# Three paddings in SBUF: where a kernel's streamed weight blocks and one operand buffer start

## Chip, cores and metric

The kernel runs on one NeuronCore of a Trainium2 chip. The metric is the device time of one execution in microseconds (us); a change is judged by runs of the kernels before and after on the same chip.

## The reference, cut to what matters

A batch of one sequence of 256 tokens, 2048 wide, passes through two blocks in float32:

```
x = first_block(x):    proj = rmsnorm(x) @ w_in                 # 2048 x 9264
                       pooled branch, sparse attention, gated merge, @ w_out
x = second_block(x):   z = rmsnorm(x) @ w_in_2                  # 2048 x 6160
                       forgetting attention + mLSTM, @ w_out_2
                       x = x + peer_ffn(rmsnorm(x))
peer_ffn:              scores = x @ w_q ...; the 16 best of 128*128 experts, 8 heads
                       act = gelu(u[idx] . x) * gate ; y = sum(act * v[idx])
```

Nearly all of the work is products of the 256 tokens with weight matrices that are read once from HBM. The expert tables `peer_u` and `peer_v` (16384 x 2048 each) are read in full: the kernel computes `gelu(x @ u.T)` for every expert, multiplies by a gate table that is zero for experts that were not chosen, and multiplies by `v`.

## The kernel before

**Arithmetic.** A float32 operand is split into a high part (an fp32r copy, made on ScalarE, line 159) and a low part (the difference, made on VectorE, line 160), and a product is three matmuls: high x high, high x low, low x high.

**Streamed blocks.** Every weight matrix comes in blocks of 128 partitions x 1024 float32 (4096 bytes in each partition, 512 KB in all). `stream()` loads one into a `wr` tile, splits it into `wh` and `wl`, and hands these to TensorE. The tiles lie in the pool "stream" (4 `wr`, 3 `wh`, 3 `wl`), and from the expert part on (line 1104, from about 1370 us) also in a second pool, "stream2": of each five blocks two then go to stream2. The pools are plain stacks in a partition, so the size of what is allocated ahead of a tile decides the address at which it starts.

**Consumers.** There are three loops over streamed blocks:

- `dense_half` (line 210; the outputs are named `mm` and `qp`): the 128x128 weights are the stationary operand, the tokens' operand (256 columns, in the big tiles `S0` to `S5`, named `S` in the profile, or in `ypp` for the pooled branch) is the moving one. A block gives 24 matmuls: 16 with `wh`, 8 with `wl`. There are 15,360 of them.
- `dense_N` (lines 193 to 195, outputs `mmn`): the tokens are stationary, the weights move, 512 columns. There are 768.
- `v_mm` (lines 1327 and 1331, outputs `y`): the gated activations `ah`, `al` are stationary, the `peer_v` block moves, 512 columns. A block gives 12 matmuls: 8 with `wh`, 4 with `wl`. There are 3072, of which 3024 have a streamed block and 48 a copy in an `S` tile.

Each matmul loads its own stationary operand; the load of the next one runs beside the matmul at hand. Between blocks of `dense_half`, other matmuls are put in: `sc` (routing scores), `rT`, and in the second half of the expert part the `G` pairs (line 1258) that build the gate table.

**Order.** The framework's scheduler orders the instructions. TensorE gets them in one queue, and the streamed blocks are loaded by one DMA queue of SyncE.

**Addresses.** Three tiles exist only to move others, or have columns that are never read: `pad` at the head of pool "stream", `pad2` at the head of the next pool ("sy", which holds `S0`, `S2`, `S3`; everything allocated later lies above it), and the first 16 columns of `ypp`. In the built program the start addresses have these remainders modulo 256 bytes:

| tile | first address before | remainder before |
|---|---|---|
| `wr`, `wh`, `wl` in stream | 21952, 38336, 50624 | 192 |
| `wr`, `wh`, `wl` in stream2 | 127808, 144192, 152384 | 64 |
| `S0` to `S5` (tokens' operands) | 62976 and up | 0 |
| `ah`, `al` (gated activations) | 189248, 199488 | 64 |
| `ypp` (its used part) | 199296 | 128 |

All steps inside these tiles from one matmul to the next are multiples of 512 bytes, so an operand keeps its remainder through a block.

Of the kernel before, what the change touches and what calls it, by code (L numbers as in the profile page):

```python
# [7 lines left out]
F32 = mybir.dt.float32  # L8
F32R = mybir.dt.float32r
# [6 lines left out]
P = 128  # L16
T = 256
# [113 lines left out]
def emit(tc, I, out):  # L131
# [5 lines left out]
    def pool(stack, name, bufs=1, psum=False, **kw):  # L137
        if psum:
            kw["space"] = bass.MemoryType.PSUM
        return stack.enter_context(tc.tile_pool(name=name, bufs=bufs, **kw))  # L140

    cp = pool(es, "const")
    ws = pool(es, "stream")

    pad = ws.tile([P, 16], F32, name="pad")
    nc.gpsimd.memset(pad, 0.0)

    def const(key, pl=None):
# [97 lines left out]
        return r[:, None, :].to_broadcast([r.shape[0], 2, T])  # L246

    sy = pool(es, "sy")
    pad2 = sy.tile([P, 16], F32, name="pad2")
    nc.gpsimd.memset(pad2, 0.0)  # L250
    es_x = ExitStack()
    sx = pool(es_x, "sx")
# [396 lines left out]

    es_m = ExitStack()  # L650
    pm = pool(es_m, "pm")
    ypp = Parts(pm.tile([P, 16 * T + 16], F32R, name="ypp")[:, 16:])
    e8 = slice(0, 8)
    split(yp, ypp.hi(e8), ypp.lo(e8))
    on = parts(2, 4)
# [30 lines left out]
    pm = pool(es_m, "pm2")  # L686
# [727 lines left out]
```

## Time and profile before

| | |
|---|---|
| time, median of 3 runs | 2917.97 us (2916.59 to 2923.99) |
| profiled execution | 2919.02 us, span 2917.2 us |
| TensorE busy | 2879.9 us, 99% of the span, 20,690 matmuls |
| VectorE, ScalarE busy | 1896.0 us (65%), 1563.2 us (54%) |
| granted TensorE clock | 0.997 of full (2.4 GHz), full in nearly every slice |
| DMA | 596 MB, mean 204 GB/s |

The matmuls are pipelined: a matmul's recorded duration (276 to 281 ns with 256 columns) is longer than the distance from its start to the next one's. In what follows, **pace** means that distance: the time between two starts in the timeline, divided by the matmuls between them.

### The profile page before, as it was taken

Reading aid. Unit: us, or ns where it says so; the run is one execution under the profiler, and the core shown is the slowest. Engines: PE = TensorE matmul, PEld = TensorE weight load, DVE = VectorE, ACT = ScalarE, POOL = GpSimd, SP = SyncE. Lnnn points to the kernel's source line nnn. Section 1 sums busy time; section 2 is a strip of 40 time slices with the busy share of each in tenths; the row PEclk is TensorE's granted clock in tenths of the full one; section 3 lists DMA queues with packets and bytes.
Section 4 is the critical chain, followed back from the end, with each engine's and each line's share of the span. In section 5 each row is a group of like instructions: output and inputs, shape, how many; then the busy total and the mean of one; then the engine's idle time right before and its main releaser. Section 6 shows DMA issues by size and latency. Waiting matters only on the chain.

```text
span 2917.2 us, 51579 instructions
## 1 busy us (share of the span) xinstructions
PE 2879.9 (99%) x20690; PEld 2690.4 (92%) x20690; DVE 1896.0 (65%) x2994; ACT 1563.2 (54%) x2463; POOL 80.7 (3%) x92
## 2 busy tenths in 40 slices
PE   8999999999999999998999999999999999999998
PEld 8998999999999899898999999999998888888887
DVE  7665666655557776566887878888645555555554
ACT  5544555544445455555444479999644444444443
POOL 0000223100000000000000000000000000000000
PEclk9999999999999999999999999999999999999999
DMA  6755444455654544444655567676866676776653
GB/s 229 239 197 187 158 151 137 165 187 184 217 186 165 181 161 163 161 160 164 229 199 210 196 238 247 237 253 239 301 226 232 242 248 221 245 247 222 245 189 114
DMA packets 197201, 596.12 MB, mean 204 GB/s; under 512 B 20832, under 2 KB 55008, under 8 KB 192736
## 3 DMA queue, kind: packets, MB, share of 16 engines
q1 hardware_dynamic: 196960, 592.82, 58.4%
q8 instruction: 162, 2.65, 0.4%
q14 instruction: 79, 0.65, 0.1%
HBM read 553.92 MB, written 35.65 MB: 202 GB/s over the span
## 4 chain that ended last, share of the span: by engine, by line
PE 97%; DVE 1%; DMA 1%; ACT 1%; issue 0%; SPq 0%; DVEq 0%; ACTq 0%
PE mm L210 58%; PE y L1327 16%; PE y L1331 8%; PE qp L210 2%; PE mmn L194 2%; PE mmn L195 2%; PE mmn L193 2%; PE G L1258 1%; PE pT L609 1%; DMA wr<-in_w_kcr 0%; PE po L193 0%; PE po L194 0%; DVE kb L405 0%; PE po L195 0%; ACT wh L159 0%
## 5 line engine op out<-in xcount | busy, mean ns | idle before, releaser
L160 DVE TENSOR_TENSOR wl<-wr,wh 128x1024 fp32r<-128x1024 f32 x976 | 1191.6, 1223 | 777.0 <-ACT wh L159 719.2
L159 ACT ACTIVATE wh<-wr 128x1024 fp32r<-128x1024 f32 x976 | 1033.0, 1061 | 1160.8 <-PE mm L210 522.6
L210 PE MATMUL mm<-S,wh 128*128 128x256 f32 x9600 | 1243.3, 280 | 11.2 <-ACT wh L159 9.3
L210 PEld LDWEIGHTS mm<-S,wh 128*128 128x128 f32 x9600 | 1173.6, 188 | 16.7 <-ACT wh L159 10.6
L210 PE MATMUL mm<-S,wl 128*128 128x256 f32 x4800 | 664.4, 279 | 0.0
L210 PEld LDWEIGHTS mm<-S,wl 128*128 128x128 f32 x4800 | 604.4, 188 | 1.8 <-issue 1.0
L1327 PE MATMUL y<-wh,al 128*128 128x512 f32 x1008 | 315.1, 393 | 0.0
L1327 PE MATMUL y<-wh,ah 128*128 128x512 f32 x1008 | 314.8, 393 | 0.0
L1331 PE MATMUL y<-wl,ah 128*128 128x512 f32 x1008 | 274.3, 393 | 0.0
L1327 PEld LDWEIGHTS y<-wh,ah 128*128 128x128 f32 x1008 | 189.1, 188 | 43.7
L1327 PEld LDWEIGHTS y<-wh,al 128*128 128x128 f32 x1008 | 189.2, 188 | 43.6
L1331 PEld LDWEIGHTS y<-wl,ah 128*128 128x128 f32 x1008 | 189.2, 188 | 43.3
L194 PE MATMUL mmn<-wl,S 128*128 128x512 f32 x256 | 102.3, 400 | 1.0 <-DVE wl L160 1.0
L195 PE MATMUL mmn<-wh,S 128*128 128x512 f32 x256 | 101.7, 397 | 0.0
L193 PE MATMUL mmn<-wh,S 128*128 128x512 f32 x256 | 97.2, 399 | 0.0
L1256 ACT ACTIVATE om<-gm,gTl 128x128 fp32r<-128x128 f32 x256 | 94.1, 398 | 0.0
L1256 ACT ACTIVATE om<-gm,gTh 128x128 fp32r<-128x128 f32 x256 | 87.6, 398 | 0.2 <-DVE gm L1248 0.2
L599 POOL TENSOR_SCALAR sm<-sm,ls 128x128 f32<-128x128 f32 (+1 forms) x64 | 77.4, 1225 | 272.5 <-DVE sc L595 143.6
L1262 ACT ACTIVATE gst<-G 128x256 f32<-128x256 f32 x128 | 81.1, 637 | 1.3
L1263 DVE TENSOR_TENSOR gst<-gst,G 128x256 f32<-128x256 f32 x128 | 76.7, 634 | 2.7 <-ACT gst L1262 2.5
L194 PEld LDWEIGHTS mmn<-wl,S 128*128 128x128 f32 x256 | 48.2, 188 | 11.7 <-DVE wl L160 1.4
L195 PEld LDWEIGHTS mmn<-wh,S 128*128 128x128 f32 x256 | 48.2, 188 | 10.6
(463 smaller groups left out, 2042.0 us busy)
## 6 DMA issues: line engine op xcount, KB each, us to landing
wr<-in_peer_u SPq DMA_DIRECT2D x256, 512.0 KB, 3.7
wr<-in_peer_v SPq DMA_DIRECT2D x256, 512.0 KB, 3.9
wr<-in_w_mg SPq DMA_DIRECT2D x64, 512.0 KB, 3.2
wr<-in_w_o SPq DMA_DIRECT2D x64, 512.0 KB, 3.2
wr<-in_w_q SPq DMA_DIRECT2D x32, 512.0 KB, 3.2
wr<-in_w_gn SPq DMA_DIRECT2D x32, 512.0 KB, 3.4
wr<-in_w_no SPq DMA_DIRECT2D x32, 512.0 KB, 3.3
wr<-in_w_pq SPq DMA_DIRECT2D x32, 512.0 KB, 3.2
```

Source lines behind the costliest of these rows:

```text
L159: se.activation(hi, src, AF.Copy)
L160: (eng or ve).tensor_tensor(lo, src, hi.bitcast(F32), op=sub)
L193: te.matmul(out_, ah, bh, start=start, stop=False, skip_group_check=True)
L194: te.matmul(out_, ah, bl, start=False, stop=False, skip_group_check=True)
L195: te.matmul(out_, al, bh, start=False, stop=stop, skip_group_check=True)
L210: te.matmul(pt, (l if i == 2 else h)[:, s], x.lo(kk) if i == 1 else x.hi(kk), start=start and i == 0 and k == 0, stop=stop and i == 2 and ...
L599: nc.gpsimd.tensor_scalar(v, v, ls[:, c:c + 1], None, op0=mult)
L1256: se.activation(om[:, t, P * i:P * i + P], o2[:, t], AF.Copy, scale=gt.bitcast(F32)[:, tk + t:tk + t + 1])
L1262: se.activation(g2, pt[:, :, 0], AF.Copy)
L1263: ve.tensor_tensor(g2, g2, pt[:, :, 1], op=add)
L1327: te.matmul(yb[tt, c + d], a[p][:, ts], w[0][d], start=i == 0 and p == 0, stop=False, **f)
L1331: te.matmul(yb[tt, c + d], a[0][:, ts], w[1][d], start=False, stop=i == P - 1, **f)
```

## The change

It gives the two pad tiles 48 instead of 16 columns, and the unused head of `ypp` 48 instead of 16. Nothing else differs. The built programs have the same instructions in the same order on TensorE, VectorE, ScalarE and SyncE; on GpSimd two memsets of the pads grow from 128x16 to 128x48.

```
-    pad = ws.tile([P, 16], F32, name="pad")
+    pad = ws.tile([P, 48], F32, name="pad")
     nc.gpsimd.memset(pad, 0.0)
...
-    pad2 = sy.tile([P, 16], F32, name="pad2")
+    pad2 = sy.tile([P, 48], F32, name="pad2")
     nc.gpsimd.memset(pad2, 0.0)
...
-    ypp = Parts(pm.tile([P, 16 * T + 16], F32R, name="ypp")[:, 16:])
+    ypp = Parts(pm.tile([P, 16 * T + 48], F32R, name="ypp")[:, 48:])
```

In the built program the tiles of pool "stream" move up by 128 bytes, and everything above by 256 bytes:

| tile | remainder before | remainder after |
|---|---|---|
| `wr`, `wh`, `wl` in stream | 192 | 64 |
| `wr`, `wh`, `wl` in stream2 | 64 | 64 |
| `S0` to `S5` | 0 | 0 |
| `ah`, `al` | 64 | 64 |
| `ypp` | 128 | 0 |

## Rows read from the trace of the kernel before

**Rows 1.** The page's first part: busy time, share of span, instructions.

```profile
PE 2879.9 (99%) x20690; PEld 2690.4 (92%) x20690; DVE 1896.0 (65%) x2994; ACT 1563.2 (54%) x2463; POOL 80.7 (3%) x92
```

**Rows 2.** Longest pieces of the chain: start us, us, what, matmuls.

```profile
183.85 20.74 PE mm L210 x183
...
556.32 283.15 PE mm L210 x2404
840.33 90.69 PE mm L210 x768
989.62 43.24 PE mm L210 x381
...
1387.34 31.14 PE mm L210 x272
...
2070.27 128.16 PE mm L210 x1128
```

**Rows 3.** Timeline of TensorE, two blocks of y: start us, us, line, operation, count.

```profile
2217.66 0.62 PE L1327 MATMUL y<-wh,ah 128*128 128x512 f32 x2
...
2220.45 0.63 PE L1327 MATMUL y<-wh,ah 128*128 128x512 f32 x2
...
2221.37 0.62 PE L1327 MATMUL y<-wh,ah 128*128 128x512 f32 x2
...
2223.18 0.62 PE L1327 MATMUL y<-wh,ah 128*128 128x512 f32 x2
```

**Rows 4.** Windows with TensorE alone: window, length, busy, matmuls, clock, DMA share.

```profile
1400.00:1710.00 310.00, 310.00 (x2711) 1.00 0.59 205
1730.00:2060.00 330.00, 330.00 (x2841) 1.00 0.70 243
2080.00:2190.00 110.00, 110.00 (x973) 1.00 0.77 268
2200.00:2880.00 680.00, 680.00 (x2947) 1.00 0.66 229
```

**Rows 5.** Windows, the matmuls of line 210 alone, in two interrupted stages.

```profile
250.00:550.00 300.00, 229.26 (x1782) 1.00 0.46 154
920.00:1360.00 440.00, 260.57 (x2117) 1.00 0.47 165
```

**Rows 6.** Timeline of TensorE, dense_N with the tokens stationary.

```profile
228.35 0.40 PE L193 MATMUL mmn<-wh,S 128*128 128x512 f32 x1
...
231.62 0.40 PE L195 MATMUL mmn<-wh,S 128*128 128x512 f32 x1
```

**Rows 7.** Timeline of TensorE where G pairs stand between blocks of dense_half.

```profile
2008.72 0.63 PE L1258 MATMUL G<-om,ah 128*128 128x256 f32 x4
2009.19 2.05 PE L210 MATMUL mm<-S,wh 128*128 128x256 f32 x16
2011.08 1.10 PE L210 MATMUL mm<-S,wl 128*128 128x256 f32 x8
2012.02 2.05 PE L210 MATMUL mm<-S,wh 128*128 128x256 f32 x16
...
2018.13 0.64 PE L1258 MATMUL G<-om,ah 128*128 128x256 f32 x4
2018.60 2.00 PE L210 MATMUL mm<-S,wh 128*128 128x256 f32 x16
2020.44 1.07 PE L210 MATMUL mm<-S,wl 128*128 128x256 f32 x8
2021.34 1.98 PE L210 MATMUL mm<-S,wh 128*128 128x256 f32 x16
```

**Rows 8.** Groups by line in 700 to 720 us: count, busy us, mean ns.

```profile
L210 PE MATMUL mm<-S,wh 128*128 128x256 f32 x81 | 10.5, 279 | 0.0
...
L210 PE MATMUL mm<-ypp,wh 128*128 128x256 f32 x32 | 4.1, 281 | 0.0
```

**Rows 9.** The pads on GpSimd: duration ns, first and last start us.

```profile
L146 POOL MEMSET pad<- x1: 111/111/111, 0.7 to 0.7; 128x16 f32 x1
```

## The prediction

> **What bounds the kernel now.** I read the page's first part, then the chain, then the timeline of TensorE. The page shows an engine that is never without work: 2879.9 us busy out of 2917.2, while VectorE stands at 65% and ScalarE at 54% [rows 1]. So no wait can be removed; only the pace of the matmuls can change. The chain shows that this pace is not one number. The same matmul, same shape, same clock, stands there in long unbroken pieces: 20.74 us for 183, which is 113.3 ns each; 283.15 us for 2404, which is 117.8; 90.69 us for 768, which is 118.1; 128.16 us for 1128, which is 113.6 [rows 2]. There are two paces, about 113.3 and 117.8 ns, and a piece keeps its own for hundreds of microseconds. The reader is to see that neither the clock (1.00 in every window [rows 4]) nor waiting makes the difference.
>
> The timeline of the last stage shows two paces side by side. A block of y that lies in pool "stream" starts at 2217.66, the next one, in stream2, at 2220.45, and the one after that, in "stream" again, at 2223.18: 2.79 us against 2.73 us for the same 12 matmuls [rows 3]. In the stream2 block the first four are still slow; the last eight take 1.81 us, 226.3 ns each, against 232.5 ns over the "stream" block. This repeats with the rotation of five blocks all through the stage: 680 us for 2947 matmuls is 230.7 ns, between the two [rows 4]. What tells the two kinds of block apart is the start address: remainder 192 in "stream", 64 in stream2, and the stationary `ah` and `al` at 64.
>
> **The change part by part.** It takes out no instruction and adds none. Two memsets grow threefold; one takes 111 ns at 0.7 us [rows 9], long before the first matmul, and I cost them at nothing; if they did delay something, twice 0.2 us. What moves is the remainder of three quarters of the streamed blocks, from 192 to 64, and of `ypp`, from 128 to 0. The offset of stationary to moving operand then is, in every loop, that of the stream2 blocks today, except in dense_N, where no streamed block has it yet. I go loop by loop; the sum is of (pace today minus fast pace) times matmuls.
>
> *The y stage.* Today 230.7, fast 226.3, over 3024 matmuls: 13.3 us. In all 98 unbroken stream2 blocks of the timeline the pace is down after four matmuls, and in all 148 unbroken "stream" blocks it is up. I take all of it. Bounds: 0 and 13.3.
>
> *dense_half, uninterrupted (556 to 931 us).* 2404 times (117.8 - 113.3) is 10.8 us, 768 times (118.1 - 113.3) is 3.7: ceiling 14.5 us [rows 2].
>
> *dense_half in the expert part.* From 1400 to 1710 us, 310 us for 2711 matmuls is 114.35 ns, 1.05 over the fast pace: 2.8 us. From 1730 to 2060, 330 us for 2841 is 116.2, 2.9 over: 8.2 us [rows 4].
>
> *dense_half between attention parts.* 1782 matmuls from 250 to 550 us and 2117 from 920 to 1360 [rows 5], of which 381 already run at 113.5 [rows 2]; most of the others run at the slow pace in the timeline. At 4.5 ns: 8.0 and 7.8 us at most.
>
> *dense_N.* From 228.35 to 231.62 us there are 14 matmuls: 233.6 ns [rows 6], 7.3 over the 226.3 of the fast y. Over 768: 5.6 us at most. No trace row shows this pairing (tokens at 0 stationary, weights at 64 moving); nearest are the y blocks, one offset fast and one slow, so I take half, 2.8.
>
> The ceilings add up to 60 us. How much of dense_half is got depends on what a remainder of 64 does there, and that is not as plain as in y. The pace is kept: both kinds of block go on at the one they are entered with if it is the fast one, and other matmuls put in between reset it. The rows show three things. After a G pair a stream2 block can stay slow to its end (2009.19: 16 in 1.89 us, 118 ns, then 8 in 0.94), and the next, in "stream", stays slow too; another stream2 block (2018.60) is at 113 by its second half (8 in 0.90), and the next one in "stream" keeps that [rows 7]. Counted over the timeline from 1400 to 2070 us, blocks entered right after `sc`, `rT` or `G` come out fast in 20 of 32 cases in stream2 and in none of 46 in "stream". And `ypp` today, with weights at 192 against 128, has the offset 64 already, and is slow throughout: its blocks (281 ns recorded, beside 279 for those of the same slow piece [rows 8]) lie inside the piece at 556 us [rows 2]. Handed over slow, it stays slow. So 64 gives a way out that 192 does not, but no certain one. I take half where the row nearest is the G pair: 7.2 of 14.5, 4.0 of 8.0, 3.9 of 7.8. After `sc` all 5 of 5 recovered: 2.5 of 2.8. With G pairs at almost every block the pace is drawn anew each time, and the stream2 blocks that today rescue a slow neighbour no longer do so: 2.0 of 8.2. Against this stands the stretch from 2070 us, fast today (1128 matmuls [rows 2]); entered slow and not interrupted, it would cost 1128 x 4.5 = 5.1 us; I charge 0.45 of that, 2.3.
>
> Sum: 13.3 + 7.2 + 2.5 + 2.0 + 4.0 + 3.9 + 2.8 - 2.3 = 33.4 us. The profiled execution took 2919.0 us (span 2917.2 and 1.8 around it), 1 us over the median of the runs; 2918.0 - 33.4 is 2884.6, and I say 2885 us. What must keep up is cover: at the fast pace a block of 512 KB is wanted every 2.72 us, and from 2080 to 2190 us the DMA engines supply just that at 0.77 busy, TensorE without a gap [rows 4].
>
> A rule of the Trainium skill speaks against all this. "SBUF — State Buffer", section "Who interferes with whom", gives TensorE two independent read ports, one for the moving operand and one for the weight load, and says that "PE and ACT never wait on anyone"; by that, addresses that are legal cannot matter, and the sum is 0. The two blocks of rows 3 do not agree with it.
>
> **The rivals.**
>
> *Nothing happens (2909 to 2927 us).* The pace might go with the pool itself (its region of SBUF, or the place of a block in the rotation) and only by chance with the remainder. For: in this trace the remainder and the pool cannot be told apart for y. Against: `ypp` and the 4-block copies in `S` tiles at remainder 0 are slow in yet other regions. A second form is that the gain is eaten by waits; against it stands the window from 2080 us. It gives 2918.
>
> *y alone (2900 to 2909 us).* dense_half falls to the slow pace once, in the long uninterrupted piece as now, and 64 holds it there, as `ypp` shows. Then 13.3 us less something for dense_N: 2918 - 13.3 = 2904.7.
>
> *Everything fast (2858 to 2864 us).* All ceilings: 2918 - 60 = 2858.
>
> *Slower (2927 to 2940 us).* The slow pace sticks at 64 better than at 192. Then what is fast today turns slow: 381 + 1128 matmuls of the chain and some 555 before 210 us, of which 183 are shown, at 4.5 ns: 9.3 us; and 1400 to 1710 us from 114.35 to 117.8, 2711 x 3.45 = 9.4. Together 18.7 us, 2936.7 if y gains nothing. It decides only if y gains less than 10 of its 13.3. For it speaks the block at 2009.19; against, that no stream2 block entered fast ever became slow unless something was put in.
>
> **How the numbers follow.** Within 0.3% (8.8 us) this measurement can hardly tell a change from none. Partial take-up (2864 to 2900, centre 2885): 0.62. Everything: 0.08. y alone: 0.14. Nothing: 0.10. Slower: 0.06. So faster 0.84, same 0.10, slower 0.06. The range 2862 to 2907 leaves out part of "everything", a little of "y alone", and the last two, about 0.2; within the likeliest case alone it would be 2866 to 2899.
>
> **What would show it.** In the profile after, every y block should take 2.72 us, without the alternation of rows 3; that is the firm step. The pieces of the chain at 556 and 840 us should show 113 to 114 ns for a matmul; if they still show 117.8, the piece was entered slow and 64 held it there. The piece after the last G pair (128.16 us for 1128) should not be longer. dense_N at 226 or 233 decides the half I guessed. The prediction is wrong if y blocks stay at 2.79, or if the pace is right and the span does not follow because TensorE starts to wait for blocks.

## The result and the profile after

The changed kernel took 2883.75 us, the median of 4 runs (2882.7 to 2885.67), against 2917.28 us (4 runs, 2915.65 to 2923.99) for the kernel before on the same chip. The ratio is 0.9882, with a 95% interval of 0.9864 to 0.9899. The profiled execution took 2884.6 us, of which 2882.7 are the span.

The page's first part, of the changed kernel:

```profile
PE 2847.4 (99%) x20690; PEld 2673.1 (93%) x20690; DVE 1896.4 (66%) x2994; ACT 1559.9 (54%) x2463; POOL 80.1 (3%) x92
```

The same 20690 matmuls keep TensorE busy for 32.5 us less than in [rows 1], and VectorE's work is unchanged. Outside its busy time TensorE has 35.3 us of the span (2882.7 - 2847.4), against 37.3 before: it does not wait less, it goes faster. The chain of the changed kernel, its longest pieces that answer to [rows 2]:

```profile
181.76 20.76 PE mm L210 x183
...
549.75 272.49 PE mm L210 x2404
823.10 90.69 PE mm L210 x768
971.83 43.25 PE mm L210 x381
...
2043.84 132.85 PE mm L210 x1128
```

Each duration divided by its count is the pace. The piece of 2404 went from 117.8 to 113.3 ns, the piece of 768 stayed at 118.1, and the piece of 1128, fast before at 113.6, is now slow at 117.8. So with one and the same offset, 64, in all of them, dense_half still has its two paces.

Windows of the changed kernel, TensorE alone (length, busy, matmuls, clock, DMA share, GB/s), which answer to [rows 4]:

```profile
1400.00:1710.00 310.00, 310.00 (x2728) 1.00 0.63 209
1730.00:2060.00 330.00, 330.00 (x2849) 1.00 0.73 246
2080.00:2190.00 110.00, 110.00 (x882) 1.00 0.67 228
2200.00:2840.00 640.00, 640.00 (x2826) 1.00 0.70 235
```

y goes at 640 / 2826 = 226.5 ns. The kernel before has 2774 matmuls in the same window, 230.7 ns. The window of 2080 us, still without a gap, now holds the slow piece and the beginning of y. In the stretch with the G products almost nothing was won: 115.8 ns for a matmul against 116.2. The next rows are the matmuls of line 210 alone, in the two stages of [rows 5]:

```profile
250.00:550.00 300.00, 231.07 (x1824) 1.00 0.49 155
920.00:1360.00 440.00, 257.38 (x2117) 0.99 0.50 165
```

The timeline of y, of the changed kernel (start us, us, line, operation, count), no longer alternates as in [rows 3]. Block follows block at 2.72 us, whichever pool the block lies in:

```profile
2214.61 0.62 PE L1327 MATMUL y<-wh,ah 128*128 128x512 f32 x2
...
2217.33 0.62 PE L1327 MATMUL y<-wh,ah 128*128 128x512 f32 x2
...
2220.05 0.62 PE L1327 MATMUL y<-wh,ah 128*128 128x512 f32 x2
```

dense_N, in the timeline, starts its 14 matmuls within 3.20 us, 228.6 ns each against 233.6 in [rows 6]:

```profile
224.87 0.39 PE L193 MATMUL mmn<-wh,S 128*128 128x512 f32 x1
...
228.07 0.39 PE L195 MATMUL mmn<-wh,S 128*128 128x512 f32 x1
```

The timeline around the G products, in the place of [rows 7], shows what has become of dense_half there:

```profile
1997.83 0.63 PE L1258 MATMUL G<-om,ah 128*128 128x256 f32 x4
1998.29 2.05 PE L210 MATMUL mm<-S,wh 128*128 128x256 f32 x16
2000.18 1.10 PE L210 MATMUL mm<-S,wl 128*128 128x256 f32 x8
...
2003.95 0.64 PE L1258 MATMUL G<-om,ah 128*128 128x256 f32 x4
2004.42 2.00 PE L210 MATMUL mm<-S,wh 128*128 128x256 f32 x16
2006.25 1.07 PE L210 MATMUL mm<-S,wl 128*128 128x256 f32 x8
2007.16 1.98 PE L210 MATMUL mm<-S,wh 128*128 128x256 f32 x16
2008.97 1.07 PE L210 MATMUL mm<-S,wl 128*128 128x256 f32 x8
2009.88 0.63 PE L1258 MATMUL G<-om,ah 128*128 128x256 f32 x4
2010.35 2.05 PE L210 MATMUL mm<-S,wh 128*128 128x256 f32 x16
```

From start to start (the recorded ends overlap), the first block behind the first G group takes 1.89 us for 16 matmuls, 118 ns: slow. Behind the second group the 8 of `wl` are down to 0.91 us, and the next block takes 1.81 for 16: fast. The third group is followed by a slow one again (2.05 us in the record, like the first). Counted over the timeline, the 63 pieces of dense_half behind G groups that are long enough to tell go fast, slow, fast, slow, in strict turn (between the first two fast ones stand 7 matmuls alone, at 117.6 ns); the last piece, of 1128, comes as a slow one.

### The profile page after: what moved, and what is told of

Its sections match the earlier page's. It is cut to its first block, busy times and chain, and to the rows that moved or that the text cites. A ratio compares the mean times of both kernels' runs of the same rounds, so it can differ in the third digit from the quotient of the medians.

```text
span 2882.7 us, 51579 instructions
## 1 busy us (share of the span) xinstructions
PE 2847.4 (99%) x20690; PEld 2673.1 (93%) x20690; DVE 1896.4 (66%) x2994; ACT 1559.9 (54%) x2463; POOL 80.1 (3%) x92
## 4 chain that ended last, share of the span: by engine, by line
PE 96%; DVE 2%; DMA 1%; ACT 1%; issue 0%; SPq 0%; DVEq 0%; ACTq 0%
PE mm L210 57%; PE y L1327 16%; PE y L1331 8%; PE qp L210 2%; PE mmn L194 2%; PE mmn L195 2%; PE mmn L193 2%; PE G L1258 1%; PE pT L609 1%; DMA wr<-in_w_kcr 0%; DVE wl L160 0%; PE po L194 0%; PE po L193 0%; DMA rsw<-rraw 0%; ACT wh L159 0%
## 5 line engine op out<-in xcount | busy, mean ns | idle before, releaser
L210 PE MATMUL mm<-S,wh 128*128 128x256 f32 x9600 | 1233.2, 279 | 10.1 <-ACT wh L159 8.1
```

Of the source, the lines that this page charges most:

```text
L210: te.matmul(pt, (l if i == 2 else h)[:, s], x.lo(kk) if i == 1 else x.hi(kk), start=start and i == 0 and k == 0, stop=stop and i == 2 and ...
```

## The experiments

**Offset or address.** The theory: the pace goes with the distance, modulo 256 bytes, between the start of the stationary and of the moving operand ("offset" in all that follows; dense_half has the weights stationary). The rival: it goes with the remainder of the streamed block itself, which the change sets to 64. Three kernels tell them apart, each the kernel before with these paddings:

```
                       pad  pad2  ypp
before                  16    16   16
changed kernel          48    48   48
e1_pad2_ypp             16    48   48
e2_pad_only             48    16   16
e3_no_ypp               48    48   16
```

The first has the changed kernel's offsets, with every remainder 128 bytes away from the changed kernel's:

```
-    pad2 = sy.tile([P, 16], F32, name="pad2")
+    pad2 = sy.tile([P, 48], F32, name="pad2")
-    ypp = Parts(pm.tile([P, 16 * T + 16], F32R, name="ypp")[:, 16:])
+    ypp = Parts(pm.tile([P, 16 * T + 48], F32R, name="ypp")[:, 48:])
```

> pad stays at 16 columns; pad2 and ypp get 48. Streamed blocks of pool stream start at 192 as before, those of stream2 now at 192, S at 128, ah and al at 192, ypp at 128: every absolute remainder differs from the change's, every offset of stationary to moving operand is the change's (64 in dense_half, 0 in y). Theory 1 (the offset sets the pace): 2884 us within 4, all y blocks 2.72 us. Theory 2 (a streamed block must itself lie at 64): no block does, so y runs at 232.5 to 233 ns throughout, 2917 to 2925 us.

It took 2887.46 us (4 runs, 2882.98 to 2890.47); ratio 0.9886, interval 0.987 to 0.9903, the changed kernel's within the measurement. Its chain:

```profile
557.58 272.49 PE mm L210 x2404
830.92 87.29 PE mm L210 x768
...
2049.76 132.85 PE mm L210 x1128
```

and its window of y:

```profile
2200.00:2840.00 640.00, 640.00 (x2825) 1.00 0.71 237
```

The piece of 2404 and the slow last piece are those of the changed kernel to 0.01 us, from other addresses, and y has 2825 matmuls in the window where the changed kernel has 2826 and the kernel before 2774. The piece of 768 is fast here (113.7 ns).

The second moves the streamed blocks to remainder 64 without a change of the offsets that dense_half and y have in the kernel before, since everything behind pool "stream" moves with them:

```
-    pad = ws.tile([P, 16], F32, name="pad")
+    pad = ws.tile([P, 48], F32, name="pad")
```

> Only pad gets 48 columns. Streamed blocks of pool stream start at 64 as in the change, but everything above moves by the same 128 bytes, so every offset is that of before. Theory 1 (the offset sets the pace): 2917 us within 4, y blocks alternate 2.79 and 2.73 us. Theory 2 (a streamed block must itself lie at 64): the blocks in stream are fast, those in stream2 (now at 192) slow; three of five blocks instead of two are fast, 2895 to 2912 us.

It took 2919.16 us (10 runs, 2916.41 to 2924.17); ratio 1.0004, interval 0.9994 to 1.0014. Its windows have 2773 matmuls of y in 640 us (2774 before), and its chain has the piece of 2404 slow and the last one fast, as in [rows 2]:

```profile
555.59 281.50 PE mm L210 x2404
837.95 90.69 PE mm L210 x768
...
2067.63 128.16 PE mm L210 x1128
```

So the rival falls: without a change of offset, moving the blocks to remainder 64 wins nothing in y or in the time. One part does not follow from the offset. The 1.65 us that its first piece is shorter than before are the 384 matmuls on `ypp`, at 113.5 ns here and 117.7 ns in the kernel before (counted over the timeline), with the same offset, 64, in both kernels: at 64 either pace can come. There is one profile of each, so it stays open whether the addresses, which are 128 bytes apart, or the execution decided here.

The third leaves only `ypp` out of the change, so that its matmuls lie at offset 192 amid others at 64:

```
-    ypp = Parts(pm.tile([P, 16 * T + 48], F32R, name="ypp")[:, 48:])
+    ypp = Parts(pm.tile([P, 16 * T + 16], F32R, name="ypp")[:, 16:])
```

> The change without its third line: ypp stays at 128 with the weights at 64, offset 192 for 384 of the 2404 matmuls of the long piece. Theory 1: offset 192 keeps a fast pace that it is entered with, so 2884 us within 3 and the piece at 113.4 ns for a matmul. Rival: the switch of offset inside the piece resets the pace, and the piece after the first ypp block runs at 117.8: up to 10 us slower, 2894 us.

It took 2886.05 us (2884.32 to 2887.44); ratio 0.9885, interval 0.9868 to 0.9901. The piece of 2404 in its chain is 1.76 us longer than the changed kernel's:

```profile
552.80 274.25 PE mm L210 x2404
827.91 87.30 PE mm L210 x768
```

and its timeline shows where:

```profile
700.66 2.05 PE L210 MATMUL mm<-ypp,wh 128*128 128x256 f32 x16
...
703.48 2.04 PE L210 MATMUL mm<-ypp,wh 128*128 128x256 f32 x16
...
706.31 1.98 PE L210 MATMUL mm<-S,wh 128*128 128x256 f32 x16
708.13 1.07 PE L210 MATMUL mm<-S,wl 128*128 128x256 f32 x8
```

The two blocks on `ypp` take 5.65 us for 48 matmuls, 117.7 ns; the block on `S` behind them is fast at once (16 in 1.82 us). All 384 matmuls at 192 are slow in this kernel, and the ones at 64 around them fast. That an offset handed over at the fast pace keeps it, as the prediction had it, is wrong: a change of offset can end the fast pace, and another one brings it back.

**Other offsets.** Is 64 a good offset, or is it only better than 192? Four kernels (s0_offset0, s128, s96, s32) scan it. `pad2` moves the tokens and everything behind them, and a pad at the head of stream2 keeps that pool at the same offset as "stream"; y then has its operands at offset 0, as in the changed kernel. The sizes are 64 and 48 columns for offset 0, 32 and 16 for 128, 40 and 8 for 96, 56 and 56 for 32. For offset 0, against the kernel before:

```
-    pad2 = sy.tile([P, 16], F32, name="pad2")
+    pad2 = sy.tile([P, 64], F32, name="pad2")
     more[:] = [pool(es_e, "stream2", **bt), 4, 2]
+    pad3 = more[0].tile([P, 48], F32, name="pad3")
+    nc.gpsimd.memset(pad3, 0.0)
```

> Weights against tokens' operands at offset 0 in dense_half (pad2 of 64 columns), y blocks against ah and al at 0 (a pad of 48 columns at the head of stream2). Theory 1: y gains its full 13 us as in the change; dense_half at offset 0 has no row so far. If offset 0 is as good in dense_half as it is in y (leaves the slow pace within four matmuls), nearly all of dense_half is fast: 2865 us. If it holds the slow pace: 2900 us or more.

> Offset 128 in every dense_half block that was at 192 before, y and dense_N at offset 0. With offset 0 the 256-column matmuls went at about 120 ns throughout and the kernel took 2957.75 us. Theory A (only the distance from offset 0 counts, 128 is the farthest): dense_half at 113.3 ns nearly everywhere, so the 24 us that the changed kernel still has above that pace are gone: about 2860 us, the chain's 2404-matmul piece 272 us and its 1128-matmul piece 128 us. Theory B (the offset counts modulo 128): about 120 ns throughout again, 288 us and 135 us for the two pieces, about 2956 us. Theory C (64 and 192 are alike and 128 is like them, two paces drawn anew after interruptions): 2880 to 2900 us.

> Offset 96 in dense_half, y and dense_N at 0. If the pace changes gradually with the offset away from 0 and 128, 96 is as good as or better than 64: about 2860 to 2884 us, 2404-matmul piece at most 272.5 us. If a multiple of 64 is what the fast pace needs, 96 goes at 118 to 120 ns throughout: 284 to 288 us for that piece, about 2935 to 2956 us.

> Offset 32 in dense_half, y and dense_N at 0. If the pace changes gradually with the distance from 0: between the 120 ns of offset 0 and the mixture of offset 64, about 2900 to 2950 us. If a multiple of 64 is what counts: like 96, 2935 us or more. If any offset other than 0 does: about 2884 us.

(dense_N, with the tokens stationary, is at the reverse of dense_half's offset: at 0 in the first of the four only, at 128, 160 and 224 in the others, not at 0 as three of these expectations say. The 384 matmuls on `ypp` stand 128 away from the others' offset.)

They took 2957.75, 2949.91, 2941.22 and 2943.36 us, one run each. The piece of 2404 matmuls in their chains, in this order, and of the first also the last piece:

```profile
564.37 287.95 PE mm L210 x2404
...
2114.82 135.36 PE mm L210 x1128
```

```profile
567.04 286.12 PE mm L210 x2404
```

```profile
561.38 285.30 PE mm L210 x2404
```

```profile
564.88 285.06 PE mm L210 x2404
```

That is 119.8, 119.0, 118.7 and 118.6 ns for offsets 0, 128, 96 and 32 in the first piece, and the last piece is slow in all four (135.36, 133.86, 133.86 and 133.48 us). As means of a piece, all are above even the slow pace of 64 and 192, 117.8 ns (single stretches go below it: the `ypp` blocks of s96, at offset 224, take 116.7 ns by the timeline). Of those tried, 113.3 ns is reached for long only at 64 and 192. The theory that only the distance from 0 counts falls (128 would be best), and so does a gradual change from 0 to 64.

The first of them also shows that what is worst for 256 columns is best for 512. In a window of y its matmuls take 226.5 ns, at the very offset at which dense_half takes 119.8:

```profile
2300.00:2840.00 540.00, 540.00 (x2384) 1.00 0.72 240
```

**What turns the pace over.** The changed kernel's last piece is slow at an offset that can be fast. My first thought was the prediction's: an interruption draws the pace anew. Six added matmuls of 128 columns, ahead of that piece and behind the last G group, should draw again (kernel f6_flip, and f6_timed, which is the same once more):

```
         jobs.append((2.6, lambda t4=t4: g_quad(t4)))
+
+    def six():
+        pt = side_bank("six")
+        for a in range(2):
+            mm3(pt[:, P * a:P * a + P], kyh[:, a], kyl[:, a], kyh[:, 1 - a], kyl[:, 1 - a], True, True)
+
+    jobs.append((0.7, six))
```

> The changed kernel's paddings, and six added 128-column matmuls right behind the last pair of G products, ahead of the 1128 matmuls of the last uninterrupted dense_half piece, whose pace is slow in the changed kernel (117.8 ns, 132.85 us). Theory: an interruption draws the pace of what follows anew, and 128-column matmuls were followed by the fast pace in 14 of 15 cases: the piece takes 128.2 us at 113.3 ns, about 4.7 us less, and the kernel about 2880 us (the six matmuls cost under 1 us). Rival: the offset and the blocks of this stage fix the pace, whatever came before: 132.85 us again, and 2884 us.

> The kernel with the six added matmuls once more, timed in rounds: its one look gave 2877.38 us and a 1128-matmul piece of 127.90 us. If that is the piece's gain and no accident, 2876 to 2881 us; if the 768-matmul piece (87.30 us there, 90.69 us in the changed kernel) varies from run to run, up to 3.4 us more in some.

One run gave 2877.38 us; the 4 later ones gave 2882.34 (2880.42 to 2884.04), ratio 0.9871, interval 0.9856 to 0.9886. The two pieces in the chain of the second:

```profile
828.41 90.69 PE mm L210 x768
...
2048.28 127.90 PE mm L210 x1128
```

The last piece is fast both times, 4.95 us shorter than in the changed kernel; so its pace hangs on what stands ahead of it. Whether such matmuls draw, turn over or set the pace, this does not tell. The timelines of the eight profiles with the changed kernel's streamed offset tell it for like matmuls, those of `sc` between 1400 and 1660 us: behind groups of six the pace is fast 96 times of 96, four times from slow, and behind the two groups of five it is turned over each time, from fast to slow 8 times and from slow to fast 8 times. That is no drawing, and six do not turn the pace over there; but the added six have other operands. By the time the gain of the last piece cannot be told from the changed kernel (intervals overlap), because other pieces vary between executions by some microseconds: the piece of 768 is 87.30 us in the first run's profile and 90.69 here. It starts behind a wait of 0.87 us for VectorE's `g`, in all kernels alike, and among the profiles with the changed kernel's offset in it it is slow in two (this one and the changed kernel's own) and fast in all others.

The strict turn behind the G groups speaks against drawing. G's own operands lie at offset 0 in both kernels, amid dense_half at 64. So I moved only them: the tile of `om` is made 64 columns longer and `om` begins at its column 48, while y's `al`, which uses the same buffers, begins at 0. No instruction is added, removed or moved on TensorE. Against the changed kernel (kernel g64):

```
-            om = pv[0].tile([P, 2, T], F32R, tag="al", bufs=GRP // 2 + 1, name="om")
+            om = pv[0].tile([P, 2 * T + 64], F32R, tag="al", bufs=GRP // 2 + 1, name="om")[:, 48:48 + 2 * T].rearrange("p (t c) -> p t c", t=2)
...
-            al = pv.tile([P, 2, T], F32R, tag="al", bufs=GRP // 2 + 1, name="al")
+            al = pv.tile([P, 2 * T + 64], F32R, tag="al", bufs=GRP // 2 + 1, name="al")[:, :2 * T].rearrange("p (t c) -> p t c", t=2)
```

> The changed kernel's paddings, and besides the G products' moving operand 192 bytes further on in its buffer, so that their stationary operand lies 64 past it, as in dense_half (0 in the kernel before and in the changed one); y's operands keep offset 0, no instruction is added or moved. In the changed kernel the 63 pieces of dense_half behind G products go at the fast and the slow pace in strict turn (F S F S ...), and so does the last piece (slow). Theory: the G products at offset 0 run against the step of the others and throw it over; at offset 64 they fit in, no piece turns, and the 7.1 us of 1725 to 2070, 0.9 us in the G products and 4.7 us of the last piece go: about 2871 us (2868 to 2876), its 1128-matmul piece 128 us. Rival: any interruption throws it over, whatever its offset: F and S in turn again, 2884 us.

It took 2875.11 us (5 runs, 2869.68 to 2875.82); ratio 0.9848, interval 0.9835 to 0.9862, which lies just under the changed kernel's (each against the kernel before as it was timed beside it; the windows below are the firmer evidence). It is the fastest of all that were run. Its timeline around G groups:

```profile
2000.67 0.62 PE L1258 MATMUL G<-om,ah 128*128 128x256 f32 x4
2001.13 1.98 PE L210 MATMUL mm<-S,wh 128*128 128x256 f32 x16
2002.94 1.07 PE L210 MATMUL mm<-S,wl 128*128 128x256 f32 x8
2003.85 1.98 PE L210 MATMUL mm<-S,wh 128*128 128x256 f32 x16
...
2006.57 0.62 PE L1258 MATMUL G<-om,ah 128*128 128x256 f32 x4
2007.02 1.98 PE L210 MATMUL mm<-S,wh 128*128 128x256 f32 x16
```

Every block is at 113 ns, behind every G group (16 in 1.81 us), and all 63 pieces are fast by the timeline; the rival, that any interruption turns the pace over, falls. To see whether 64 is needed or only something other than 0 and its like, the number 48 in the added slice became 16 (G at offset 192, kernel g192) and 32 (G at 128, kernel g128):

> As the kernel with the G products at offset 64, but at 192 (their moving operand 64 bytes on in its buffer). Theory: what throws the neighbours over is an offset that differs from theirs; at 192 the G products shift the step too, and fast and slow pieces of dense_half come in some mixture: 7 to 12 us above the version at 64, 2877 to 2884 us. Rival: only offset 0 (and its like, 128) throws it over, any odd multiple of 64 fits in: no slow piece, 2868 to 2876 us.

> As the kernel with the G products at offset 64, but at 128, where dense_half itself went at 118 to 120 ns in most of its matmuls. Both theories: like 0, pieces throw over, 2877 to 2884 us. If 128 leaves all pieces fast, only offset 0 does it: 2868 to 2876 us.

These took 2897.91 and 2887.53 us, one run each. The window from 1730 to 2030 us with TensorE alone, for G at 0 (the changed kernel), at 64, at 192 and at 128:

```profile
1730.00:2030.00 300.00, 300.00 (x2592) 1.00 0.72 245
```

```profile
1730.00:2030.00 300.00, 300.00 (x2649) 1.00 0.73 250
```

```profile
1730.00:2030.00 300.00, 300.00 (x2549) 1.00 0.71 240
```

```profile
1730.00:2030.00 300.00, 300.00 (x2588) 1.00 0.72 243
```

That is 115.7, 113.3, 117.7 and 115.9 ns for a matmul. With G at 192, all pieces behind G groups but the first are slow by the timeline; at 128 fast and slow come in strict turn, as at 0. So the G products were worth more in what they did to their neighbours than in their own 256 matmuls, and of the four offsets tried only the neighbours' own leaves them alone. That 192 is worse than 0 was expected by neither theory. Of the 28.2 us by which g192's run lies above g64's profiled one (2869.68 us), this stretch and the last piece make some 17: the stretch lasts 303.9 us in g64 up to its last piece, 2683 matmuls at 113.25 ns, and 2683 x 4.4 is 11.8; the piece takes 132.85 against 127.84 us, 5.0. Most of the rest (10.1 us) lies ahead of 1656 us, in parts that the two kernels share, and is not explained by the offsets of G.

One rival for the strict turn at 0 and 128 is not tested: by the code, the G groups write two pairs of PSUM banks in turn, and each pair might set a pace of its own. One place in the changed kernel's timeline speaks against it. The eighth G matmul, one of eight that stand singly among those of dense_half, is followed at 1700.89 us by 16 matmuls in 1.81 us, fast; the G group at 1709.56 us, which by the order of the code has the same pair of banks, is followed at 1710.03 us by 16 in 1.88 us, slow. The two `sc` groups of five speak against it too, since each was followed by the fast pace in four profiles and by the slow one in four.

## Why the prediction was right, and where only its sum was

The time, 2885 us, was met to 1.3 us, and the likeliest case (partial take-up) is what happened. Term by term, by the same views:

- **y**: 13.3 us predicted, (230.7 - 226.5) x 3024 = 12.7 measured. All of it, as said; the firm step held.
- **dense_half, uninterrupted**: 7.2 predicted as half of two pieces, 10.7 measured: the whole of one (283.15 - 272.49) and nothing of the other. "Handed over slow, it stays slow" did not decide the long piece: it was fast from its start, in every profile with this offset. The pace of the second piece was open, and varied between executions.
- **From 1400 to 1710 us**: 2.5 predicted, (114.35 - 113.64) x 2711 = 1.9 measured. "After `sc` all 5 of 5 recovered" did not hold: the group of five ahead of 1403.95 us turned fast into slow for 168 matmuls, 168 x 4.4 = 0.7 us.
- **From 1730 to 2060 us**: 2.0 predicted, (116.16 - 115.83) x 2841 = 0.9 measured. Here the step itself failed: "the pace is drawn anew each time". Fast and slow come in strict turn, so that half of the pieces are slow for certain, as long as the G products stand at offset 0 between matmuls at 64. g64 shows what the change left lying there.
- **The last piece**: 2.3 of loss predicted, 4.7 measured (132.85 against 128.16), and the same 132.85 in e1_pad2_ypp and e3_no_ypp, which have these offsets too: with strict turns it was decided, and the 0.45 of the price that was charged had no row behind it. It becomes fast by the six matmuls of f6_flip, or by G at 64.
- **Between the attention parts**: 4.0 and 3.9 predicted. By the windows of line 210, 229.26 / 1782 against 231.07 / 1824 is 1.97 ns, 3.5 us; 260.57 / 2117 against 257.38 / 2117 is 3.2. Right to a fraction.
- **dense_N**: 2.8 predicted, a half by a guess. In the rows shown it is 5.0 of the 7.3 ns; counted over the timeline (excess of each start-to-start distance under 300 ns over 226.7 ns), 5.66 us before and 2.93 after, so 2.7 us. Some of its pieces stay slow.

Together 12.7 + 10.7 + 1.9 + 0.9 + 3.5 + 3.2 + 2.7 - 4.7 = 30.9 us, of 34.4 between the two profiled executions (2919.0 and 2884.6). Of the missing 3.5 us, 2.1 lie ahead of the piece that starts at 181.76 us (183.85 in [rows 2]), where waits at the kernel's beginning are a little shorter; the rest is not assigned. That the sum came within 1.3 us was in part luck, because its errors had both signs: the long piece paid for the turning-over that the prediction had not seen.

"Nothing happens" is refuted by the time, and its reason, the pool, by the y blocks, which take 2.72 us in either pool. e1_pad2_ypp and e2_pad_only together show that the gain goes with the offset and not with the remainder. "Slower" would have needed 64 to hold the slow pace better than 192; the scan shows 64 and 192 as the only two of six offsets with the fast pace, and the long piece went from slow at 192 to fast at 64. The rule of the Trainium skill ("SBUF — State Buffer", section "Who interferes with whom": two independent read ports of TensorE, and an engine that never waits on anyone), read as the prediction read it, does not agree with these runs: the same matmul, at a clock of 1.00 and with no wait, takes 113.3 or 119.8 ns by its two addresses alone. The section speaks of engines that share a port and names no address. Why the paces are these was not shown; nothing here looks into the reads.

## What to carry to other kernels

When TensorE is never idle, divide the chain's long pieces by their counts: two paces for one shape at one clock mean that something besides the work sets the pace, here, in the main, the distance modulo 256 bytes between the two operands' start addresses. Set it for each loop by itself (64 for 256 moving columns, 0 for 512, in this kernel), and see that short interrupting matmuls have the same offset as the loop that they interrupt, since they can leave thousands of others slow. Look for strict turns in a timeline before calling something a draw.

## What the runs showed of the hardware

At a granted clock of 1.00, 32-bit matmuls of 128x128 by 256 columns start every 113.3, 117.8 or up to 119.8 ns, and those by 512 columns every 226.5 or about 233 ns, in the main by the offset between the operands. Offset 0 is the worst of those tried for 256 columns and is fast for 512. At 64 both paces exist, and one of them can last for 2404 matmuls. Behind groups of four matmuls at offset 0 or 128, fast and slow come in strict turn (with 0 over 62 or 63 pieces in each of five profiles, of four kernels; with 128 in one); behind groups of four at 192 all is slow (one profile), and behind four at 64 all is fast (one profile). Behind groups of five 128-column matmuls the pace was turned over 16 times of 16, and behind groups of six it was fast 96 times of 96. At 192 inside 64, 384 matmuls were slow and those around them fast. A piece that starts behind a wait of 0.87 us had either pace, with no difference that the profile shows.
